# Three-part chains, 512-column builds and an earlier place for the gate tiles in the SSM stage of a hybrid encoder step

## The chip, the cores and the metric

The kernel runs on one core of a Trainium2 chip. The metric is the device time of one execution in microseconds (us), the median of several runs. TensorE multiplies matrices, VectorE (DVE in the rows) and GpSimd (POOL) work elementwise, ScalarE (ACT) does activations and copies out of PSUM, and SyncE (SP) issues the DMAs.

## The reference, cut to what matters

One layer is applied to 1024 prompt tokens and 32 sample tokens, together 1056. After a modulated RMS norm a single wide projection gives all inputs of two branches. Branch A is a state-space model (SSM) with 32 groups of 16 channels and 64 complex states each, branch B a sparse attention whose indexer picks up to 256 keys a query. Both branches are gated and merged.

```
u, zs, q, k, v, za, qi, ki, wi, gm = jnp.split(z, offs, axis=-1)
ys, hr, hi = ssm_scan(us, h_re, h_im, disc, c_re, c_im, d_skip)   # h' = a h + b u ; y = Re(c h) + d u
ys = jax.nn.gelu(ys)
ys = ys * jax.nn.sigmoid(ys @ w_glu + b_glu)                      # GLU
ys = ys * jax.nn.silu(zs)
...                                                               # indexer, top-k selection, attention -> ya
merged = sigmoid(g_s) * (ys @ w_ps) + sigmoid(g_a) * (ya @ w_pa)  # g_s, g_a = split(gm)
out = merged @ w_o
```

## The kernel before, in words

Every large product is made in three passes over operands split in two exact parts (lines 458 to 460: high by high, low by high, high by low). `ztile` (line 464) makes 128 columns of the wide projection: it loads 512 KB of weights (line 204), splits them into a high part by a cast on ScalarE (line 46) and a low part by a subtraction on GpSimd (line 49), and runs 3 groups of 24 matmuls of 352 columns, each followed by its evacuation. The tiles of the projection differ in that evacuation alone: `uproj` (SSM input, ScalarE copies), `gate_tile` (one ScalarE tanh a group, line 490, and a store to DRAM, line 491), and `silu_tile` (a ScalarE tanh and then a VectorE product, lines 483 and 484, and a store, line 486). There are 16 gate tiles, 4 silu tiles of the SSM branch and 4 of the attention branch.

The SSM stage works in four quarters of 8 groups. `build(q)` makes the matrices of a quarter: ER and EI on VectorE (`lin`, lines 546 to 548), G2 on VectorE for quarter 0 and on GpSimd for the others (lines 558 to 560), then transposes to Bc (lines 573, 574), small products to Ksb (lines 582 to 584) and shifts to Tq (lines 589 to 593). Tokens stand in 133 chunks of 8. `chain(q)` multiplies chunk inputs Uq by Bc (line 607, "input products"), copies the result to vv (line 613), runs the rotation, the scan over chunks and the rotation back on VectorE (lines 619 to 644), which ends in the states HS, and then makes the output Yq from Uq by Tq and HS by G2 (lines 654 to 656), its gelu (lines 659 to 664) and a store to yD (line 665). vv and HS have the tag "hs" with one buffer, so they share one place in memory. Input products and output products take their PSUM tiles from one pool of two buffers (`ps_s`).

The GLU loads yD into yg (line 704), splits it (line 706) and multiplies. Behind it stand the gate tiles up to NS, the indexer, the gate tiles from NS to NI, the first `prep` of the attention, four silu tiles, the gate tiles from NI to NG, the selection of the keys on VectorE and ScalarE (lines 1001 to 1060), and the attention; gate tile 15 comes from the list `gates` inside the attention.

The instructions of an engine don't stand in the order of the text: a planner lays them out at build time by priority (the order of the text) and by its own estimate of what is ready. Each engine then runs its list strictly in order. So gate tiles 0 to 4, whose text follows the GLU, lie on TensorE ahead of it.

Of the kernel before, what the change touches and what calls it, by code (L numbers as in the profile page):

```python
# [7 lines left out]
F32 = mybir.dt.float32  # L8
# [4 lines left out]
ALU = mybir.AluOpType  # L13
PSUM = bass.MemoryType.PSUM
DRAM = bass.MemoryType.DRAM
# [7 lines left out]
NCH = 133  # L23
NST = 134
QT = [(i * 128, 128, 128 * (i + 1)) for i in range(8)]
NS, NI, NG = 5, 10, 15
# [8 lines left out]
def body(nc, tc, I, O, dbg=None):  # L35
# [3 lines left out]
    te, ve, se, ge, sp = nc.tensor, nc.vector, nc.scalar, nc.gpsimd, nc.sync  # L39
# [448 lines left out]
    def gate_tile(f):  # L488
        tg = stg.tile([128, NT], F32, tag="stg", name="tg")
        ztile(C_GM + 128 * f, 128, lambda n, ps: se.activation(tg[:, ns(n)], ps, AF.Tanh, scale=0.5))  # L490
        sp.dma_start(thD[f], tg)

# [17 lines left out]
    xq = stX.enter_context(tc.tile_pool(name="xq", bufs=1, side="right", reuse_waits="tile"))  # L510
    fl = lambda t, k: t[:, k].rearrange("p a b -> p (a b)")

    P1, P2 = (xq.tile([128, 2, 16, 8], F32, name=n) for n in ("P1", "P2"))
    C1, C2 = (xq.tile([128, 2, 16, 16], F32, name=n) for n in ("C1", "C2"))
    for e in range(2):
        r = slice(64 * e, 64 * e + 64)
        for d in range(2):
            o = slice(64 * d, 64 * d + 64)
# [9 lines left out]
    def build(q):  # L528
# [13 lines left out]
        def lin(eng, out, a, b, c, d, op):  # L542
            for k in range(4):
                e1, e2 = (xq.tile([128, 16, 8], F32, name="e" + x, tag="e" + x + ("v" if eng is ve else "g"), bufs=2)
                          for x in "12")
                eng.tensor_tensor(e1, a[:, k], b[:, k], op=ALU.mult)
                eng.tensor_tensor(e2, c[:, k], d[:, k], op=ALU.mult)
                eng.tensor_tensor(out[:, k], e1, e2, op=op)
# [4 lines left out]
        e3 = [128, 16, 8]  # L553
        for g in range(8):
            k, e = 4 * q + g // 2, g % 2
            e1, e2 = (xq.tile(e3, F32, name="e" + x, tag="e" + x + ("v" if eng is ve else "g"), bufs=2) for x in "12")
            for o, pt_, ct in ((e1, P1, C1), (e2, P2, C2)):
                eng.tensor_tensor(o, pt_[:, e, k].unsqueeze(1).to_broadcast(e3),
                                  ct[:, e, k].unsqueeze(2).to_broadcast(e3), op=ALU.mult)
            eng.tensor_tensor(G2[:, g], e1, e2, op=ALU.add)  # L560
# [35 lines left out]
    def chain(q, ops):  # L596
        Uq, G2, Bc, Tq = ops
        pr = slice(4 * q, 4 * q + 4)
# [10 lines left out]
        vv = xq.tile([128, 2, 4, NST], F32, name="vv", tag="hs")  # L609
        for c in range(2):  # L610
            for e in range(2):
                s_ = slice(64 * (c ^ e), 64 * (c ^ e) + 64)
                se.copy(vv[64 * e:64 * e + 64, c, :, 0:NCH], va[e][s_].rearrange("p (k c) -> p k c", k=4)[:, :, 0:NCH])
        vr4, vi4 = vv[:, 0, :, 0:NCH], vv[:, 1, :, 0:NCH]
# [33 lines left out]
        Yq = xq.tile([128, 8, NCH], F32, name="Yq", tag="uy", bufs=2)  # L648
# [19 lines left out]
    ops = build(0)  # L668
    for q in range(4):
        if q < 3:  # L670
            uproj(q + 1)
        nxt_ = build(q + 1) if q < 3 else None
        chain(q, ops)
        ops = nxt_
    for q in range(4):
        silu_tile(C_ZS + 128 * q, zsD[q])
# [31 lines left out]
    for q in range(4):  # L708
# [5 lines left out]
        for n in range(3):  # L714
            c = ns(n)
# [8 lines left out]
    for f in range(NS):  # L724
        gate_tile(f)
    stG.close()

# [543 lines left out]
```

## Time and profile before

| what | us |
|---|---|
| median of 3 runs (range) | 1136.44 (1135.09 to 1136.77) |
| span of the profiled execution | 1134.5 |
| TensorE matmul busy in it | 1032.5 (91%) |
| VectorE busy | 806.0 (71%) |
| SSM stage, from the first build to the last store of yD | about 106 to 282 |
| GLU | 299 to 329 |
| indexer scores, last one | to 466 |
| selection of the keys, to the first softmax | 466 to 673 |
| attention | 673 to 972 |

A row of the profile gives time in us from the start of the span and the duration of one instruction, or for a group its busy time and mean. "Idle" is what an engine waited ahead of an instruction, with what released it. PEclk is the clock granted to TensorE as a share of full speed. Matmuls are pipelined, so their durations overlap; the step from one start to the next is the time that one costs.

### The profile page before, as it was taken

What the parts mean: (1) busy time and instruction counts of PE and PEld (TensorE: products, weight loads), DVE (VectorE), ACT (ScalarE), POOL (GpSimd) and SP (SyncE); (2) the same over time, 40 slices, a digit from 0 to 9 for tenths busy, and PEclk for the clock granted to TensorE, in tenths of its full rate; (3) what the DMA queues carried; (4) which work ended last, traced back from release to release, by engine and by line L of the source; (5) the groups of instructions that cost most, each with busy time, mean ns of one, the idle gap of its engine ahead of it and who ended that gap; (6) DMA issues with size and microseconds to landing.
All of it is one profiled execution on the core that took longest, in us unless ns stands there. A gap on an engine that the chain in (4) does not pass through costs nothing.

```text
span 1134.5 us, 17585 instructions
## 1 busy us (share of the span) xinstructions
PE 1032.5 (91%) x6298; PEld 950.9 (84%) x6298; DVE 806.0 (71%) x2001; ACT 540.3 (48%) x1141; POOL 348.1 (31%) x407
## 2 busy tenths in 40 slices
PE   7788989899799999988899969999997799999996
PEld 5477888899699889978889968999896599998775
DVE  4899986633435554899999996776857976687433
ACT  2542351343434554878778125555676666334111
POOL 2456645732412010224223203321325711220000
PEclk9999999999899999989999979999999999999999
DMA  9915121332651011333222322232243342754321
GB/s 275 231 41 153 39 58 58 115 87 88 199 155 51 22 37 59 94 95 76 81 81 95 111 80 66 75 95 57 66 120 102 106 138 86 225 175 146 122 64 51
DMA packets 128074, 115.53 MB, mean 102 GB/s; under 512 B 13500, under 2 KB 109200, under 8 KB 127988
## 3 DMA queue, kind: packets, MB, share of 16 engines
q1 hardware_dynamic: 127752, 114.36, 34.7%
q8 instruction: 50, 0.82, 0.3%
q14 instruction: 36, 0.29, 0.1%
q10 hardware_dynamic: 236, 0.06, 0.0%
HBM read 79.55 MB, written 30.08 MB: 97 GB/s over the span
## 4 chain that ended last, share of the span: by engine, by line
PE 50%; DVE 33%; ACT 6%; DMA 6%; issue 4%; SPq 1%; POOL 0%; DVEq 0%; POOLq 0%; ACTq 0%
PE pz L458 8%; PE pz L459 8%; PE pz L460 8%; DVE junk L1007 5%; ACT junkb L1005 3%; PE psm L1240 3%; PE psm L1242 3%; PE psm L1241 3%; PE pss L891 3%; PE pt L947 2%; DMA xt<-in_x_prompt 1%; PE pspo L957 1%; PE pss L786 1%; PE pss L787 1%; PE pspo L956 1%
## 5 line engine op out<-in xcount | busy, mean ns | idle before, releaser
L458 PE MATMUL pz<-hH,wh 128*128 128x352 f32 (+1 forms) x1080 | 356.6, 331 | 18.6 <-DVE zt L484 11.5
L459 PE MATMUL pz<-hL,wh 128*128 128x352 f32 (+1 forms) x1080 | 355.4, 329 | 0.1
L460 PE MATMUL pz<-hH,wl 128*128 128x352 f32 (+1 forms) x1080 | 355.4, 329 | 0.0
L49 POOL TENSOR_TENSOR wl<-raw,wh 128x1024 fp32r<-128x1024 f32 (+1 forms) x69 | 153.1, 2220 | 297.1 <-ACT wh L46 256.2
L458 PEld LDWEIGHTS pz<-hH,wh 128*128 128x128 f32 (+1 forms) x1080 | 205.7, 191 | 25.5 <-DVE zt L484 13.5
L459 PEld LDWEIGHTS pz<-hL,wh 128*128 128x128 f32 (+1 forms) x1080 | 205.7, 190 | 2.8 <-issue 0.8
L460 PEld LDWEIGHTS pz<-hH,wl 128*128 128x128 f32 (+1 forms) x1080 | 205.7, 190 | 1.9 <-issue 0.8
L1007 DVE TENSOR_SCALAR_CACHE_REDUCE junk<-sco,thra 128x1024 bf16<-128x1024 f32 (+2 forms) x96 | 96.7, 1008 | 0.4
L46 ACT CAST wh<-raw 128x1024 fp32r<-128x1024 f32 (+2 forms) x53 | 46.5, 878 | 61.7 <-PE pz L459 52.0
L895 ACT ACTIVATE Sm<-Sm,mx 128x128 f32<-128x128 f32 (+8 forms) x68 | 52.9, 777 | 44.1 <-DVE mx L892 43.7
L794 DVE SCALAR_TENSOR_TENSOR sco<-rl,wi,sco 128x384 f32<-128x384 f32 (+6 forms) x49 | 47.9, 987 | 35.0 <-ACT rl L789 34.1
L1005 ACT ACTIVATE junkb<-sco,thrb 128x896 bf16<-128x896 f32 x64 | 59.8, 934 | 19.7 <-DVE keepc L1020 10.5
L789 ACT ACTIVATE rl<-pss 128x384 f32<-128x384 f32 (+6 forms) x56 | 40.6, 737 | 49.0 <-PE pss L787 44.0
L892 DVE CUSTOM_DVE_ANT_0 Sm<-pss,mb 128x512 f32<-128x512 f32 (+4 forms) x68 | 39.9, 592 | 32.5 <-PE pt L947 27.6
L949 ACT CAST PH<-pt 128x512 fp32r<-128x512 f32 (+2 forms) x96 | 44.3, 479 | 38.0 <-PE pt L947 19.0
L950 DVE TENSOR_TENSOR PL<-pt,PH 128x512 fp32r<-128x512 f32 (+2 forms) x96 | 51.6, 550 | 8.4 <-ACT PH L949 7.1
L1242 PE MATMUL psm<-o,mL 128*128 128x512 f32 (+1 forms) x144 | 56.6, 395 | 0.0
L1240 PE MATMUL psm<-o,mH 128*128 128x512 f32 (+1 forms) x144 | 56.5, 394 | 0.0
L1241 PE MATMUL psm<-o,mH 128*128 128x512 f32 (+1 forms) x144 | 56.4, 394 | 0.0
L891 PE MATMUL pss<-kH,qs 128*128 128x512 f32 (+2 forms) x96 | 36.5, 382 | 15.1 <-DVE mx L892 14.7
L947 PE MATMUL pt<-idf,Sm 128*128 128x128 f32 x288 | 45.4, 276 | 3.3 <-DVE PL L950 3.1
L1005 ACT ACTIVATE junkb<-sco,thrc 128x384 bf16<-128x384 f32 x64 | 43.6, 681 | 7.2 <-DVE thrc L1023 3.9
(444 smaller groups left out, 2246.9 us busy)
## 6 DMA issues: line engine op xcount, KB each, us to landing
raw<-in_w_in SPq DMA_DIRECT2D x44, 512.0 KB
thD<-tg SPq DMA_DIRECT2D x16, 528.0 KB
wm<-in_w_mod SPq DMA_DIRECT2D x16, 512.0 KB
tgl<-thD SPq DMA_DIRECT2D x24, 176.0 KB
tgl<-thD SPq DMA_DIRECT2D x8, 528.0 KB
kd<-zf SPq DMA_DIRECT2D x32, 128.0 KB
raw<-in_w_mod SPq DMA_DIRECT2D x8, 512.0 KB
rawo<-in_w_o SPq DMA_DIRECT2D x8, 512.0 KB
```

The costliest lines, as they stand in the source:

```text
L49: leng.tensor_sub(l, src, f32(h))
L458: te.matmul(ps, wh, xh, start=first, stop=False)
L459: te.matmul(ps, wh, xl, start=False, stop=False)
L460: te.matmul(ps, wl, xh, start=False, stop=last)
L891: te.matmul(S[:m, :w], lhsT, r[:, c], start=t == 0, stop=t == len(rhs) - 1)
L895: se.activation(Sm[:m, :nk], Sm[:m, :nk], AF.Exp, scale=-1.0, bias=mx[:m, last:last + 1], accum_out=rs[:m])
L947: te.transpose(pt[:, (k - b0) * 128:(k - b0 + 1) * 128], P[:, k * 128:(k + 1) * 128], idf)
L1005: se.activation(junkb[:m, :nk], x[:m], AF.Sign, bias=t, accum_out=self.cnt[:m, k:k + 1])
L1007: ve.tensor_scalar(junk[:m, :nk], x[:m], t, None, op0=ALU.is_ge, op1=ALU.add, accum_out=self.cnt[:m, k:k + 1])
L1240: te.matmul(ps, mh, wh, start=first, stop=False)
L1241: te.matmul(ps, mh, wl, start=False, stop=False)
L1242: te.matmul(ps, ml, wh, start=False, stop=last)
```

## The change

The builds use whole 512-column operands where four 128-column instructions stood; each sum is made in place, the first product being written into the target. `chain` is cut into `chain_in` (input products and vv), `chain_scan` (VectorE part to HS) and `chain_out` (output products, gelu, store). The loop now runs scan(q), build(q+1), chain_in(q+1), chain_out(q), where it ran build(q+1), then the whole chain(q). vv has a buffer of its own, Yq has one buffer where it had two. Gate tiles 0 to 5 stand ahead of the silu tiles; before, gate tiles 0 to 4 stood behind the GLU. Gate tiles 6 to 10 (before 5 to 9) stand behind the indexer, 11 to 14 (before 10 to 14) ahead of the selection. Nothing else changes but comments.

```diff
-NS, NI, NG = 5, 10, 15
+NS, NI, NG = 6, 11, 15
...
         def lin(eng, out, a, b, c, d, op):
-            for k in range(4):
-                e1, e2 = (xq.tile([128, 16, 8], F32, name="e" + x, tag="e" + x + ("v" if eng is ve else "g"), bufs=2)
-                          for x in "12")
-                eng.tensor_tensor(e1, a[:, k], b[:, k], op=ALU.mult)
-                eng.tensor_tensor(e2, c[:, k], d[:, k], op=ALU.mult)
-                eng.tensor_tensor(out[:, k], e1, e2, op=op)
+            e2 = xq.tile(e4, F32, name="e2", tag="e2" + ("v" if eng is ve else "g"))
+            eng.tensor_tensor(out, a, b, op=ALU.mult)
+            eng.tensor_tensor(e2, c, d, op=ALU.mult)
+            eng.tensor_tensor(out, out, e2, op=op)
...
-        e3 = [128, 16, 8]
-        for g in range(8):
-            k, e = 4 * q + g // 2, g % 2
-            e1, e2 = (xq.tile(e3, F32, name="e" + x, tag="e" + x + ("v" if eng is ve else "g"), bufs=2) for x in "12")
-            for o, pt_, ct in ((e1, P1, C1), (e2, P2, C2)):
-                eng.tensor_tensor(o, pt_[:, e, k].unsqueeze(1).to_broadcast(e3),
-                                  ct[:, e, k].unsqueeze(2).to_broadcast(e3), op=ALU.mult)
-            eng.tensor_tensor(G2[:, g], e1, e2, op=ALU.add)
+        for e in range(2):
+            e2 = xq.tile(e4, F32, name="e2", tag="e2" + ("v" if eng is ve else "g"))
+            for o, pt_, ct in ((G2[:, e::2], P1, C1), (e2, P2, C2)):
+                eng.tensor_tensor(o, pt_[:, e, pr].unsqueeze(2).to_broadcast(e4),
+                                  ct[:, e, pr].unsqueeze(3).to_broadcast(e4), op=ALU.mult)
+            eng.tensor_tensor(G2[:, e::2], G2[:, e::2], e2, op=ALU.add)
...
-    def chain(q, ops):
+    def chain_in(q, ops):
...
-        vv = xq.tile([128, 2, 4, NST], F32, name="vv", tag="hs")
+        vv = xq.tile([128, 2, 4, NST], F32, name="vv")
...
+        return vv
+
+    def chain_scan(q, vv):
+        pr = slice(4 * q, 4 * q + 4)
...
-        Yq = xq.tile([128, 8, NCH], F32, name="Yq", tag="uy", bufs=2)
+        return HS
+
+    def chain_out(q, ops, HS):
+        Uq, G2, Bc, Tq = ops
+        Yq = xq.tile([128, 8, NCH], F32, name="Yq")
...
     ops = build(0)
+    vv = chain_in(0, ops)
     for q in range(4):
         if q < 3:
             uproj(q + 1)
-        nxt_ = build(q + 1) if q < 3 else None
-        chain(q, ops)
+        HS = chain_scan(q, vv)
+        if q < 3:
+            nxt_ = build(q + 1)
+            vv = chain_in(q + 1, nxt_)
+        chain_out(q, ops, HS)
         ops = nxt_
+    for f in range(NS):
+        gate_tile(f)
     for q in range(4):
         silu_tile(C_ZS + 128 * q, zsD[q])
...
-    for f in range(NS):
-        gate_tile(f)
     stG.close()
```

## Rows read from the trace of the kernel before

**Rows 1.** The page: busy time by engine, and the span in 40 slices.
```profile
PE 1032.5 (91%) x6298; PEld 950.9 (84%) x6298; DVE 806.0 (71%) x2001; ACT 540.3 (48%) x1141; POOL 348.1 (31%) x407
PE   7788989899799999988899969999997799999996
DVE  4899986633435554899999996776857976687433
```
**Rows 2.** Busy time by stretch: length, PE, PEld, DVE, ACT, POOL, PEclk, DMA, GB/s.
```profile
104.00:130.00 26.00, 20.59 (x132) 19.39 (x131) 25.92 (x90) 8.20 (x20) 18.82 (x35) 0.87 0.13 42
130.00:165.00 35.00, 31.23 (x219) 30.43 (x218) 32.04 (x83) 13.78 (x39) 15.05 (x22) 0.95 0.12 40
282.00:308.00 26.00, 17.97 (x98) 16.32 (x97) 11.44 (x11) 11.97 (x14) 11.87 (x5) 0.80 0.71 220
466.00:640.00 174.00, 158.79 (x957) 154.51 (x956) 168.81 (x513) 129.19 (x298) 53.19 (x34) 0.97 0.29 84
```
**Rows 3.** Waits of TensorE from 104 to 330: total us, times, longest.
```profile
PE pt L573 <- DVE ER L548: 5.4, 1, 5.4
PE pz L458 <- DVE zt L484: 4.9, 2, 4.2
PE pss L458 <- ACT wh L46: 4.3, 1, 4.3
PE pss L460 <- DVE wl L49: 3.7, 1, 3.7
PE pt L589 <- DVE Ksb L584: 2.7, 1, 2.7
PE pss L655 <- DVE HS L643: 2.6, 2, 1.7
PE pt L573 <- DVE EI L548: 2.3, 4, 1.0
```
**Rows 4.** Chain that ended last, from the last SSM quarter to the GLU: start, us.
```profile
249.35 0.62 DVE w L619
...
263.90 0.72 PE pss L655 x4
...
281.64 0.36 SPq L665
282.10 7.41 DMA yg<-yD
289.58 8.36 ACT ygH L46 x7
```
**Rows 5.** Timeline between quarters 1 and 2 of the chain: start, us, engine.
```profile
200.70 0.39 PE L655 MATMUL pss<-HS,G 128*128 128x133 f32 x2
203.97 1.98 PE L607 MATMUL pss<-Uq,Bc 128*128 128x133 f32 x16
207.63 0.73 DVE L619 TENSOR_TENSOR w<-vv,TCt 128x532 f32<-128x532 f32 x1 [3.04 <-ACT vv L613]
...
225.04 0.71 DVE L644 TENSOR_TENSOR HS<-gr,gi 64x536 f32<-64x536 f32 x1
```
**Rows 6.** Timeline of TensorE in the GLU.
```profile
305.23 0.50 PE L458 MATMUL pss<-ygH,wh 128*128 128x352 f32 x1
305.52 0.50 PE L459 MATMUL pss<-ygL,wh 128*128 128x352 f32 x1
```
**Rows 7.** Timeline of TensorE around the end of the selection.
```profile
663.08 0.32 PE L459 MATMUL pz<-hL,wh 128*128 128x352 f32 x1
663.24 0.32 PE L460 MATMUL pz<-hH,wl 128*128 128x352 f32 x1
672.95 0.80 PE L891 MATMUL pss<-kH,qs 128*128 128x512 f32 x1 [9.39 <-DVE mx L892]
```
**Rows 8.** Groups from 105 to 300, shapes apart: count, busy us, mean ns.
```profile
L558 POOL TENSOR_TENSOR e<-P,C 128x128 f32<-128x128 f32 x47 | 31.0, 687 | 1.2 <-DVE C L522 1.2
L560 POOL TENSOR_TENSOR G<-e,e 128x128 f32<-128x128 f32 x24 | 15.8, 678 | 0.2
L662 POOL TENSOR_TENSOR a<-a,Yq 128x532 f32<-128x532 f32 x8 | 10.7, 1332 | 0.5
L548 DVE TENSOR_TENSOR ER<-e,e 128x128 f32<-128x128 f32 x16 | 6.0, 403 | 2.6 <-PE pt L582 2.6
L619 DVE TENSOR_TENSOR w<-vv,TCt 128x532 f32<-128x532 f32 x4 | 3.3, 824 | 3.0 <-ACT vv L613 3.0
```
**Rows 9.** Timeline of one collision of VectorE with GpSimd.
```profile
107.06 2.38 POOL L49 TENSOR_TENSOR wl<-raw,wh 128x1024 fp32r<-128x1024 f32 x1
107.17 2.42 DVE L546 TENSOR_TENSOR e<-RR,BR 128x128 f32<-128x128 f32 x1
```
**Rows 10.** Timeline of ScalarE: second groups of two gate tiles, then two groups of prep(1).
```profile
629.04 0.47 ACT L490 ACTIVATE tg<-pz 128x352 f32<-128x352 f32 x1 [3.37 <-PE pz L460]
640.56 0.46 ACT L490 ACTIVATE tg<-pz 128x352 f32<-128x352 f32 x1 [3.32 <-PE pz L460]
...
659.76 0.45 ACT L834 COPY zf<-pz 128x352 f32<-128x352 f32 x1 [2.54 <-PE pz L460]
674.42 0.42 ACT L834 COPY zf<-pz 128x352 f32<-128x352 f32 x1
```
**Rows 11.** By tile, ER and then tg: ns min/median/max, first and last start.
```profile
L548 DVE TENSOR_TENSOR ER<-e,e x16: 275/290/1343, 111.1 to 158.1; 128x128 f32<-128x128 f32 x16
L490 ACT ACTIVATE tg<-pz x48: 437/462/469, 217.0 to 656.8; 128x352 f32<-128x352 f32 x48
```

More of the change, by code (lines that the diff above doesn't have):

```diff
@@ L594, in build @@
         return Uq, G2, Bc, Tq
-    def chain(q, ops):
+    def chain_in(q, ops):
         Uq, G2, Bc, Tq = ops
-        pr = slice(4 * q, 4 * q + 4)
         va = [ps_s("va"), ps_s("vb")]
```

## The prediction

> **What bounds the kernel now.** I read the page first: TensorE is busy for 91% of the span, and only in the slices ahead of 150 us and near 290, 490, 660 and 870 us does its share drop [rows 1]. So the end of the kernel is TensorE's work plus the time in which it waits or runs slowly, and a change in the SSM stage is worth what it removes of that lost time, not what it removes from VectorE's busy time. The busy time by stretch says which engine is late in each stage: from 104 to 130 us VectorE has no free time (25.9 of 26 us) and TensorE's clock is 0.87; from 282 to 308 us TensorE works for 18.0 of 26 us at a clock of 0.80 while no other engine reaches half; from 466 to 640 us, in the selection, VectorE has 168.8 of 174 us [rows 2]. The waits of TensorE from 104 to 330 us name what was late: two waits at the start of the GLU (4.3 and 3.7 us, together 8.0), one for a silu tile's VectorE product (4.9 us in two, the longest 4.2), one for ER (5.4), then Ksb (2.7), HS (2.6) and EI (2.3) [rows 3].
>
> The chain of waits shows why the GLU is late. The last output products of the chain begin at 263.9, the store of yD is issued at 281.6, its way through DRAM takes 7.4 us and the splits on ScalarE 8.4 us [rows 4]. So from HS to the GLU's first matmul some 34 us pass (264 to 298), and the last scan decides when. The period of the quarters comes from the timeline: output products of quarter 1 end at 200.7, input products of quarter 2 follow at 204.0, and its scan begins at 207.6 after VectorE has stood for 3.0 us [rows 5]. vv waits for HS's place and the input products for the PSUM tiles that the output products hold.
>
> **The change, part by part.** The sum is made against the profiled span, 1134.5 us; the median of the runs is 1.9 us above it, and I add that at the end.
>
> *Chains in three parts, vv apart from HS.* This takes the output products, the gap and the input products out of the ring that connects one scan to the next. The scan of quarter 2 begins at 207.6 and ends with HS at 225.8 [rows 5], that of quarter 3 begins at 249.4 [rows 4]: a period of 42 us, of which the scan is 18. What stays in the ring is the scan, the next build's VectorE part (six instructions of 0.82 us, 5 us, [rows 8]) and, where it isn't done by then, part of the copy to vv. I estimate a period of 24 to 28 us, so that the last scan ends 42 to 54 us earlier (three periods, each 14 to 18 us shorter) and yD is split well before 270. What is late next is TensorE itself: it has ten projection tiles to run there. So the two GLU waits go, 8.0 us [rows 3]; between 0, if the period does not shrink, and 8.0 I take 8.0, since even a period shorter by only 5 us (three periods, 15 us) brings the splits 15 us forward and the extra tile below lasts 11.5. The slow matmuls behind these waits go with them: starts are 0.29 us apart there [rows 6], about double the 0.16 us apart at 663 [rows 7], and over some 15 matmuls that is 2.0 us. What the split adds: Yq has one buffer, so the copies of the next quarter wait for the store of this one, 7.4 us by the yD transfer [rows 4] against a period of over 20; nothing.
>
> *Builds in 512 columns.* VectorE runs 96 instructions of 128 columns for ER and EI, at 403 ns in the row shown, and 24 such for G2 of quarter 0; 24 and 6 of 512 columns replace them. The nearest row is the 532-column product at 824 ns [rows 8]: 96 times 0.40 is 38, 24 times 0.82 is 20, so 18 us of VectorE time leave the stretch 104 to 165. GpSimd has 71 instructions for G2 in the trace, 31.0 and 15.8 us together; 18 of the 532-column kind at 1.33 us [rows 8] are 24 us instead of 47. Both are off TensorE's path except where TensorE waits for ER, EI, Ksb: 10.4 us [rows 3]. Of the 5.4 us for ER I take nothing, since the first transposes now wait for three whole 512-column instructions (3 times 0.82, 2.5 us, and one collision of 2.4 us [rows 9], about the 5 us of today). Of Ksb and EI together, 5.0 us, between 0 and 5.0, I take half, 2.5, because they stand in VectorE's list behind scans and shorter builds halve the queue but don't empty it. The clock dips in the two stretches to 165 us, 0.87 and 0.95 [rows 2], lose 26 times 0.13 plus 35 times 0.05, 5.1 us; they follow the waits, so I take 1.5 of it.
>
> *Gate tiles ahead of silu tiles.* A gate tile leaves PSUM through ScalarE alone, a silu tile needs VectorE, whose list runs in order and holds scans. With gates as the filler of the scans the longest wait of this kind goes, 4.2 us [rows 3], and I keep 0.7 for silu tiles that run beside the last scan; bounds 0 and 4.9. The silu tiles now end just ahead of the GLU, so the stores of zsD and the loads of z2 on SP's queue lie closer; the GLU needs z2 one quarter at a time and the first quarter's store is three tiles old by then, so nothing.
>
> *One gate tile moves from the selection to the SSM stage.* It brings one 512 KB load, one cast, one GpSimd split of 2.4 us (a collision with VectorE that the period's slack covers), 72 matmuls, three tanhs and a store. On TensorE a tile takes 11.5 us (640.56 less 629.04) [rows 10]. In the SSM stage this is work, not loss. In the selection it leaves 11.5 us of TensorE time free, and TensorE already stands for 9.4 us there until the first softmax [rows 7], because VectorE sets the end of that stage. The first group of the next prep's K tile runs ahead of that stand and the second at 674 [rows 10], so 48 matmuls of that tile (7.6 us) and the next tile can fill the hole, if the planner puts them there. Bounds: 0 if all is filled, 11.5 if nothing is. It was already placing such work there, so I take 3.0.
>
> Sum: 8.0 + 2.0 + 2.5 + 1.5 + 4.2 = 18.2 us less lost time, 3.0 given back: 15.2. The span becomes 1119.3, and with 1.9 the time **1121 us**.
>
> **The rivals.** *Longer GpSimd instructions hold up VectorE.* A VectorE product that starts 0.1 us behind a GpSimd split of 2.38 us takes 2.42 us and ends with it [rows 9], where such products have a mean of 0.4 [rows 8]. If every one of the 18 GpSimd products of 1.33 us does this to an instruction that TensorE waits for, the four kinds of waits on ER, EI, Ksb and HS, eight in number [rows 3], grow by up to 0.9 us each (1.33 less the 0.4 of a 128-column one), 7.5 us, and the 4.0 us taken for Ksb, EI and clock are gone too: 1121 + 11.5, about **1133**. Against it: the total that GpSimd holds falls from 47 to 24 us. The Trainium skill, "SBUF — State Buffer", section "SBUF: two separate sides", says that the port pair shared by the two engines is an exclusive lock held for a whole instruction; by that rule fewer and longer holds mean rarer but worse waits, and the trace agrees with the lock (2.42 against 2.38 us).
>
> *The hole in the selection stays open* (the slower side). The planner may leave TensorE without the K tile there. Then the full 11.5 us are lost against whatever the SSM stage gives back; it decides from the point where the SSM stage gives less than 11.5. If only the GLU waits of 8.0 go, the time is 1136.4 - 8.0 + 11.5, **about 1140**. For it speak the present stand of 9.4 us, which the planner did not foresee, and VectorE's full stretch there [rows 2], which fixes the length of the selection whatever TensorE does.
>
> *The planner makes nearly the same plan.* Gate tiles whose text stood behind the GLU already ran ahead of it, from 217 us, and the last of the four builds has its ER by 158 us, 90 us ahead of its scan [rows 11]. If the order of text decides little, the tile and the waits change places and the time stays at **1135 to 1138**.
>
> *More goes.* If VectorE's 18 us in 104 to 165 also shorten the ER wait and all dips, another 5.4 + 3.6 + 2.5, and the hole is filled: **1107**.
>
> **How the numbers follow.** Forecast 0.52 (1113 to 1128), port 0.16, hole 0.17, same plan 0.09, more 0.06. The range 1109 to 1141 takes in the forecast's bounds, the port and the hole and leaves out the far ends of the last two. A difference under about 0.2% (2.3 us) can't be told from none, so faster means below 1134.2 and slower above 1138.7. Faster: 0.52 + 0.16 + 0.06 = 0.74; same 0.09; slower 0.17.
>
> **What would show it.** In the profile of the changed kernel: vv of quarter q+1 copied before the scan of quarter q ends; scans 22 to 30 us apart; the last yD store before 250; no TensorE wait for the GLU's operands; gate tanhs between about 120 and 210, and no TensorE wait on a silu product over 1 us; the first softmax 10 to 18 us earlier than 673, and more than one group of prep(1)'s K tile ahead of it. I am wrong if the first softmax isn't earlier, or if it is and TensorE's stand ahead of it has grown to 15 us or more; or if scans stay 35 us apart, which would mean that memory or PSUM, not the order, sets the period.

## The result, and the profile after

The changed kernel takes 1145.51 us (median of 4 runs, 1144.66 to 1146.52) where the kernel before takes 1136.33 us in the runs beside it: a ratio of 1.0075, with a 95% interval from 1.0054 to 1.0095. The forecast was 1121 us with a range of 1109 to 1141, so the sign is wrong and the time lies above the range. The profiled execution has a span of 1142.8 us, 8.3 us more than the 1134.5 us of before.

The page of the changed kernel, the busy time by engine and the slices of TensorE and VectorE, hardly differs from [rows 1]:

```profile
PE 1039.4 (91%) x6298; PEld 954.5 (84%) x6298; DVE 815.6 (71%) x1911; ACT 541.9 (47%) x1142; POOL 335.4 (29%) x352
...
PE   7878888988999999988989969899997899999997
...
DVE  4899898814334564799999996776858976587433
```

The same 6298 matmuls run, so the question is where they wait or run slowly. Busy time by stretch of the kernel after (columns as in [rows 2]), with the selection shifted by the 10 us that it now comes later:

```profile
104.00:130.00 26.00, 16.12 (x102) 15.77 (x102) 23.14 (x37) 4.99 (x10) 14.15 (x14) 0.80 0.13 42
130.00:165.00 35.00, 31.79 (x233) 31.10 (x232) 34.50 (x56) 16.98 (x44) 17.48 (x18) 0.98 0.21 65
...
285.00:330.00 45.00, 44.97 (x281) 43.79 (x280) 17.53 (x23) 10.64 (x20) 6.24 (x3) 1.00 0.37 121
476.00:650.00 174.00, 158.78 (x958) 154.46 (x957) 169.14 (x516) 130.33 (x299) 51.85 (x33) 0.97 0.29 85
```

VectorE executes 37 instructions from 104 to 130 us instead of the 90 of [rows 2] and is still busy for 23.1 us of the 26. From 104 to 165 us VectorE is busy for 57.6 us where it was for 58.0. TensorE has lost in the first of these stretches: it is busy for 16.1 us instead of 20.6, at a granted clock of 0.80 instead of 0.87. The GLU, in the stretch from 285 us, now runs without a gap at full clock (44.97 of 45 us), where [rows 2] had a clock of 0.80. The selection is as full of VectorE as before (169.1 against 168.8 us). So the forecast gain at the GLU came, and something as large went elsewhere. The waits of TensorE from 104 to 330 us (total, times, longest), to be read beside [rows 3]:

```profile
PE pt L569 <- DVE rh L630: 9.9, 1, 9.9
PE pss L657 <- ACT Yq L659: 6.1, 3, 3.0
PE pt L585 <- DVE Ksb L580: 3.2, 1, 3.2
PE pz L458 <- DVE zt L484: 3.1, 1, 3.1
PE pt L569 <- ACT vv L608: 1.4, 1, 1.4
PE pss L658 <- DVE HS L642: 0.4, 1, 0.4
```

Both waits of 4.3 and 3.7 us at the GLU are gone and those on HS nearly so. In their place stand one wait of 9.9 us ahead of the first transposes of ER (5.4 before) and three on the copies to Yq, 6.1 us, which did not exist. Together the waits listed make 24.1 us; those of [rows 3] made 25.9.

The three-part chain itself did what it should. The last HS comes at 228.1 us (264.6 before), the last store of yD is issued at 251.5 (281.6, [rows 4]), and the scans end at 147.5, 178.0, 201.8 and 228.1. But nothing behind it is earlier, as the marks of the two executions show (us; "tile matmuls left" are those 352-column matmuls of the projection tiles, of 3240 in all, that have not started by the first softmax):

| mark | before | after | difference |
|---|---|---|---|
| last matmul of the GLU | 328.0 | 336.6 | +8.6 |
| last indexer score | 465.9 | 476.1 | +10.2 |
| first softmax | 672.6 | 680.5 | +7.9 |
| first product of the attention branch of the merge | 975.9 | 981.9 | +6.0 |
| end of the span | 1134.5 | 1142.8 | +8.3 |
| tile matmuls left at the first softmax | 600 | 551 | -49 |
| from the first softmax to the end | 461.9 | 462.3 | +0.4 |

The GLU ends 8.6 us later because exactly 72 more tile matmuls, one gate tile of 11.5 us, have run ahead of its end (1056 against 984) and only 2.9 us were gained against that. And the last two lines are the other half: by the first softmax 49 more matmuls are done, at 0.16 us each [rows 7] 7.8 us of TensorE time, and the rest of the kernel takes as long as before.

### The profile page after: what moved, and what is told of

It is laid out like the page before. It is cut to its first block, busy times and chain, and to the rows that moved or that the text cites. A ratio compares the mean times of both kernels' runs of the same rounds, so it can differ in the third digit from the quotient of the medians.

```text
span 1142.8 us, 17424 instructions
## 1 busy us (share of the span) xinstructions
PE 1039.4 (91%) x6298; PEld 954.5 (84%) x6298; DVE 815.6 (71%) x1911; ACT 541.9 (47%) x1142; POOL 335.4 (29%) x352
## 4 chain that ended last, share of the span: by engine, by line
PE 54%; DVE 30%; DMA 6%; ACT 5%; issue 4%; POOL 1%; SPq 0%; DVEq 0%; POOLq 0%; ACTq 0%
PE pz L458 9%; PE pz L459 9%; PE pz L460 9%; DVE junk L1014 4%; PE pss L898 3%; PE psm L1247 3%; PE psm L1249 3%; PE psm L1248 3%; ACT junkb L1012 2%; DMA xt<-in_x_prompt 2%; PE pt L954 2%; PE pspo L964 1%; PE pss L793 1%; PE pss L794 1%; PE pspo L963 1%
## 5 line engine op out<-in xcount | busy, mean ns | idle before, releaser
L49 POOL TENSOR_TENSOR wl<-raw,wh 128x1024 fp32r<-128x1024 f32 (+2 forms) x69 | 153.6, 2227 | 285.0 <-ACT wh L46 268.8
L898 PE MATMUL pss<-kH,qs 128*128 128x512 f32 (+2 forms) x96 | 37.9, 396 | 18.4 <-DVE mx L899 14.7
L1230 ACT ACTIVATE tt<-xo 128x512 f32<-128x512 f32 (+1 forms) x18 | 11.4, 632 | 75.5 <-DVE xo L1228 46.4
```

The source lines that it names most:

```text
L49: leng.tensor_sub(l, src, f32(h))
L898: te.matmul(S[:m, :w], lhsT, r[:, c], start=t == 0, stop=t == len(rhs) - 1)
```

## Experiments

Two theories were put against each other. **Tile theory:** the gate tile moved ahead of the GLU costs its 11.5 us there and is not paid back where it was taken away. **Chain theory:** the new order or the longer instructions of the SSM stage cost the time. In the expectations below, "theory A" is the tile theory and "theory B" or "waits theory" the chain theory; "plan theory" says that a wait taken away is replaced by others, so that their sum stays. Ratios are to the kernel before on the same chip, with 95% intervals. Marks and waits are read from one profiled execution of each kernel. Most of these lie within 2.6 us of the median of their kernel; that of the wide builds for quarters 1 to 3 is 5.2 us above it and that of the kernel without tile 0 is 3.9 us below.

**The gate tile back in its place.** The changed kernel with the numbers of tiles of before:

```diff
-NS, NI, NG = 6, 11, 15
+NS, NI, NG = 5, 10, 15
```

> The changed kernel with gate tile counts as before (5 ahead of the silu tiles, 5 behind the indexer, tile 10 again in the selection). Theory A, the moved tile: in the changed kernel the GLU ends 8.6 us later, which is 11.5 us of one more gate tile less about 3 us of saved waits, and later stages give back only about 2 of the 11.5; so this kernel ends its indexer 10 to 12 us earlier than the changed one and measures 1135 to 1139. Theory B, the waits: the tile is work moved and is repaid by work pulled ahead of the first softmax (48 matmuls, 7.6 us); the loss comes from new TensorE waits in the SSM stage (ER 9.9, Yq 6.1, a silu product 3.1 us); so this kernel measures 1142 to 1146.

Measured: 1136.49 us, ratio 0.9984 [0.9964, 1.0003]. The whole loss is gone with this one line: from 1.0075 to 0.9984 is 0.91%, 10.3 us. The GLU ends at 323.5 us, 13.1 earlier than in the changed kernel and 4.5 earlier than before. So the rest of the change is worth 4.5 us there, where the forecast had 18.2, and at the end of the kernel not even that can be told from nothing. The first softmax comes 7.7 us earlier than before (664.9 against 672.6), with 631 tile matmuls left instead of 600, and the rest takes 7.2 us longer. Its two largest waits of TensorE in the same stretch are those of the changed kernel; of the two waits at the GLU, one is still there (3.5 us):

```profile
PE pt L569 <- DVE rh L630: 8.7, 1, 8.7
PE pss L657 <- ACT Yq L659: 5.3, 2, 2.8
PE pss L460 <- DVE wl L49: 3.5, 1, 3.5
PE pt L585 <- DVE Ksb L580: 3.2, 1, 3.2
...
PE pt L569 <- DVE EI L546: 1.2, 1, 1.2
PE pz L458 <- DVE zt L484: 0.7, 1, 0.7
PE pss L658 <- DVE HS L642: 0.4, 1, 0.4
```

**The gate tile alone moved**, in the kernel before:

```diff
-NS, NI, NG = 5, 10, 15
+NS, NI, NG = 6, 11, 15
```

> The kernel before with the gate tile counts of the change alone (6 behind the GLU in the text, 5 behind the indexer, 4 ahead of the selection). Theory A: the tile costs 11.5 us ahead of the indexer, of which the stand of 8.0 us at the GLU takes some, and little comes back: 1138 to 1146. Theory B: it is repaid: 1133 to 1138.

Measured: 1147.38 us, 1.0076 [1.0053, 1.0099]. The one line, without anything else of the change, costs 0.76%, 8.6 us. With the run before, this shows from both sides that the loss belongs to the moved tile. Its trace has the marks of the changed kernel: the GLU ends 7.1 us later than before, 551 tile matmuls are left at the first softmax, and the rest takes 465.3 us, no less than before.

**The changed kernel with the builds of before** (128-column instructions):

```diff
-            eng.tensor_tensor(out, a, b, op=ALU.mult)
-            eng.tensor_tensor(e2, c, d, op=ALU.mult)
-            eng.tensor_tensor(out, out, e2, op=op)
+            for k in range(4):
...
+                eng.tensor_tensor(e1, a[:, k], b[:, k], op=ALU.mult)
+                eng.tensor_tensor(e2, c[:, k], d[:, k], op=ALU.mult)
+                eng.tensor_tensor(out[:, k], e1, e2, op=op)
```

> The changed kernel with the builds of before in 128-column instructions. Theory B, the waits: the wait of TensorE for ER falls from 9.9 to about 5.4 us, input products of quarter 0 come some 5 us earlier, and the time falls by 4 to 7 us to 1139 to 1142. Theory A gives the builds no part in the end: 1144 to 1147.

Measured: 1144.37 us, 1.006 [1.0036, 1.0085]. The interval covers the 1.0075 of the changed kernel: inside it the width of the builds decides nothing that can be told. The wait on ER falls back from 9.9 to 5.5 us, and those on EI come to 7.7 us instead.

**The 512-column builds alone**, in the kernel before (the same edit the other way round, in `lin` and for G2):

> The kernel before with the 512-column builds alone. Theory B: the ER wait grows to about 10 us and nothing else changes, 1139 to 1142. Theory A: the builds lie beside other work, 1135 to 1138.

Measured: 1130.6 us, 0.9933 [0.9911, 0.9955], the lowest ratio of the study (the interval overlaps that of the half tiles below) and a miss for both theories, whose ranges began at 1135 and 1139. The last HS comes at 258.0 us instead of 264.6, and the GLU ends 6.0 us earlier. VectorE is busy for 50.7 us from 104 to 165 us, 7.3 less than before. This happens although TensorE's largest waits ahead of the GLU's end are

```profile
PE pt L569 <- DVE rh L627: 9.9, 1, 9.9
PE pss L458 <- ACT wh L46: 7.1, 1, 7.1
```

so the 9.9 us wait for ER belongs to the 512-column builds, not to the new chain, and the builds win in spite of it.

**The chain in three parts alone**: `chain_in`, `chain_scan` and `chain_out` with vv in its own buffer and one Yq buffer, 128-column builds, five gate tiles behind the GLU as before.

```diff
-        vv = xq.tile([128, 2, 4, NST], F32, name="vv", tag="hs")
+        vv = xq.tile([128, 2, 4, NST], F32, name="vv")
...
-        Yq = xq.tile([128, 8, NCH], F32, name="Yq", tag="uy", bufs=2)
+        Yq = xq.tile([128, 8, NCH], F32, name="Yq")
...
-        nxt_ = build(q + 1) if q < 3 else None
-        chain(q, ops)
+        HS = chain_scan(q, vv)
+        if q < 3:
+            nxt_ = build(q + 1)
+            vv = chain_in(q + 1, nxt_)
+        chain_out(q, ops, HS)
```

> The kernel before with the three-part chains, vv apart and one Yq buffer alone (builds of 128 columns, five gate tiles behind the GLU as before). Waits theory: the store of the last yD comes 25 to 35 us earlier and the GLU waits of 8.0 us go, nothing else grows: 1127 to 1132 beside a kernel before at 1136. Plan theory (each order of TensorE's list has about the same sum of waits, 22 to 26 us from 104 us to the end of the GLU, because a wait taken away lets another operand come late): GLU waits go, waits on Yq copies and builds come, 1134 to 1139.

Measured: 1141.1 us, 1.003 [1.0012, 1.0049], above both ranges. The largest term of the forecast, alone, is a loss of 0.3%, 3.4 us. The last HS is at 234.9 us, 30 us earlier than before, and the long GLU wait is gone, but the waits of TensorE are now

```profile
PE pt L573 <- DVE EI L548: 6.0, 4, 4.7
PE pt L573 <- DVE ER L548: 5.8, 2, 4.2
PE pt L589 <- DVE Ksb L584: 3.6, 2, 3.1
```

EI has grown from the 2.3 us of [rows 3] to 6.0: the builds are now late, not the scans. The GLU itself ends at 313.8 us, 14.2 earlier than before, but only because TensorE has run 98 tile matmuls fewer by then (886 against 984), which is 15.7 us of work; the first softmax comes at 672.1, as before. So an earlier GLU is no gain by itself: the work has only changed places.

**The five gate tiles ahead of the silu tiles alone:**

```diff
+    for f in range(NS):
+        gate_tile(f)
     for q in range(4):
         silu_tile(C_ZS + 128 * q, zsD[q])
...
-    for f in range(NS):
-        gate_tile(f)
```

> The kernel before with its five gate tiles ahead of the silu tiles, nothing else. Waits theory: the 4.9 us on silu products go, 1130 to 1133. Plan theory: the silu products stand closer to the GLU, whose operands are late anyway at 298 us, so TensorE has no filler left there and waits longer: 1136 to 1141.

Measured: 1137.79 us, 0.9995 [0.9982, 1.0009]: no change. The wait of 4.9 us on the silu product is gone, as forecast, and the GLU ends at 325.6 instead of 328.0. But HS has 5.4 us (2.6 in [rows 3]), and from the first softmax to the end takes 467.2 us instead of 461.9.

**The changed kernel with four gate tiles ahead of the GLU:**

```diff
-NS, NI, NG = 6, 11, 15
+NS, NI, NG = 4, 9, 15
```

> The changed kernel with four gate tiles ahead of the silu tiles and tile 9 in the selection (one tile fewer in the SSM stage than before, two fewer than the change). Tile theory: a tile ahead of the indexer costs its 11.5 us less waits, and a tile in the selection costs little as long as TensorE stands there; the GLU ends 9 to 12 us earlier than with five tiles, the selection's stand of 6 us and one group of the K tile (3.8 us) give way, so 1126 to 1132. Rival: the tile only moves and comes back whole behind the first softmax: 1135 to 1138.

Measured: 1135.19 us, 0.9969 [0.9957, 0.9982], in the range of the rival. Between four and five tiles lies 0.15% (1.7 us, and the two intervals overlap), where the sixth cost 0.91%. The first softmax comes at 656.0 us, 8.9 earlier than with five tiles; yet 683 tile matmuls are left, and the rest takes 477.4 us, 8.3 more. Here the later stage pays for each matmul that it gets.

**Five gate tiles, and Yq in two half tiles**, each stored by itself, in the changed kernel:

```diff
-        Yq = xq.tile([128, 8, NCH], F32, name="Yq")
         for g in range(8):
+            if g % 4 == 0:
+                yh = xq.tile([128, 4, NCH], F32, name="Yq", bufs=2)
...
-        sp.dma_start(yD[q].rearrange("(g m) s c -> (m s) g c", m=16), Yq)
+                sp.dma_start(yD[q].rearrange("(g m) s c -> (m s) g c", m=16)[:, g - 3:g + 1], yh)
```

> The changed kernel with five gate tiles, and Yq in two half tiles that are each stored when ready, so that a copy no longer waits for the store of the whole last quarter. If the single Yq buffer costs what TensorE waits for it (5.3 us with five gate tiles), the wait falls under 2 us and the time by 3 to 5 us: 1131 to 1134. Plan theory: the wait goes and another takes its place, 1135 to 1138.

Measured: 1132.67 us, 0.9952 [0.9936, 0.9967]. The wait on Yq is gone and the GLU starts at 263.9 us (271.7 with whole tiles). Its end moves by 0.8 us only, 322.7 against 323.5, since other waits take the place, so the 0.3% between the two kernels (their intervals touch) is not shown as a gain of the SSM stage:

```profile
PE pt L569 <- DVE rh L630: 8.7, 1, 8.7
PE pt L585 <- DVE Ksb L580: 5.5, 2, 3.2
PE pz L458 <- DVE zt L484: 4.5, 2, 2.7
```

**The 512-column builds for quarters 1 to 3 only**, in the kernel before, to take the 9.9 us wait away:

```diff
+            if q == 0:
+                for k in range(4):
+                    e1, e2 = (xq.tile([128, 16, 8], F32, name="e" + x, tag="s" + x) for x in "12")
...
+                return
```

> The kernel before with 512-column builds for quarters 1 to 3 and the 128-column build for quarter 0, whose operands TensorE waits for. If the long wait for ER (9.9 us with 512 columns throughout, 5.4 before) is a plain addition, this kernel is 3 to 5 us faster than the one with 512 columns throughout: ratio 0.988 to 0.991 to the kernel before. Plan theory: the first wait shortens and others come, ratio 0.992 to 0.997.

Measured: 1141.66 us, 1.004 [1.0021, 1.0059], a miss: 1% slower than with the wide builds everywhere. The edit is not quite the 128-column build of before: its two temporaries have one buffer each where that build had two. The wait on ER is still 8.4 us, since the first product of ER starts at 110.1 us (106.4 before), behind three copies that take 1.1, 2.5 and 1.2 us instead of 0.3 to 0.4. In the timeline of VectorE the scan of quarter 0 begins at 134.0 us (129.4 with wide builds everywhere), behind 128-column pieces of G2, and two of its instructions take 2.8 us instead of 0.7:

```profile
133.78 0.29 DVE L565 TENSOR_TENSOR G<-e,e 128x128 f32<-128x128 f32 x1
133.99 0.70 DVE L630 TENSOR_TENSOR w<-vv,TCt 128x532 f32<-128x532 f32 x1
...
135.35 2.80 DVE L632 TENSOR_TENSOR gr<-w,w 128x532 f32<-128x532 f32 x1
...
151.49 2.77 DVE L654 TENSOR_TENSOR HS<-gr,gi 64x536 f32<-64x536 f32 x1
```

Beside each of these two stands a GpSimd split, in the timeline of GpSimd:

```profile
135.07 2.50 POOL L49 TENSOR_TENSOR wl<-raw,wh 128x1024 fp32r<-128x1024 f32 x1 [4.42 <-ACT wh L46]
...
151.30 2.38 POOL L49 TENSOR_TENSOR wl<-raw,wh 128x1024 fp32r<-128x1024 f32 x1 [7.78 <-ACT wh L46]
```

That scan ends at 155.0 us instead of 147.1, the later ones follow 36 to 38 us apart (35 to 38 with the wide builds everywhere), and the last HS is 9.2 us later. That the 8 us at the first scan are the cause of the 1% was read from the traces and not tried by itself.

**The parts that had helped together**: five gate tiles, Yq in halves, 128-column build for quarter 0.

```diff
...
+            if q == 0:
+                for k in range(4):
...
+                return
```

> The changed kernel with five gate tiles, half stores of Yq, and the 128-column build for quarter 0. By plain addition the ER wait falls from 8.7 to about 5 us: ratio to the kernel before 0.990 to 0.993 (it was 0.995 with the 512-column build throughout). Plan theory: 0.994 to 0.998.

Measured: 1131.25 us, 0.9959 [0.9942, 0.9976]. It can't be told from the half tiles alone (0.9952), nor is it better than the wide builds alone.

**A gate tile left out**, once the first, which runs ahead of the GLU, and once number 14, whose text stands ahead of the selection. The kernel before computes nothing for that tile and stores zeros in its place:

```diff
-        ztile(C_GM + 128 * f, 128, lambda n, ps: se.activation(tg[:, ns(n)], ps, AF.Tanh, scale=0.5))
+        if f == 0:
+            ge.memset(tg, 0.0)
+        else:
+            ztile(C_GM + 128 * f, 128, lambda n, ps: se.activation(tg[:, ns(n)], ps, AF.Tanh, scale=0.5))
```

> The kernel before with gate tile 0 left out (its 72 matmuls, load and splits; zeros are stored in its place), a measurement of what a tile costs ahead of the indexer. Tile theory: 11.5 us of TensorE time there moves the indexer and with it the selection; the kernel is 7 to 11 us faster. Rival, that TensorE has time for one tile beside the waits of the SSM stage: 0 to 4 us faster.

Measured without tile 0: 1134.76 us, 0.9978 [0.9962, 0.9994], a gain of 2.5 us, below the 7 to 11 of the tile theory and within the 0 to 4 of the rival: what a tile costs ahead of the GLU depends on how many there are. A sixth cost 8.6 us on balance, and leaving out one of the five gives back 2.5. The wait at the head of the GLU grows,

```profile
PE pss L458 <- ACT wh L46: 14.6, 1, 14.6
```

where the two waits there made 8.0 us in [rows 3] and now make 18.3 with the 3.7 us behind it. Its first matmul is bound to the operands, which come 7.6 us earlier (the last split ends at 290.5 instead of 298.1), not 11.5. The GLU ends 7.8 us earlier and the first softmax comes 12.7 us earlier; then 4.9 us are lost again up to the attention branch of the merge, with 631 matmuls left.

> The kernel before with gate tile 14 left out, the last ones of the selection, and zeros stored in its place: what a tile costs there. Tile theory: VectorE sets the length of the selection, the K tile of the next prep is pulled ahead, and the attention has a floor at about 600 tile matmuls behind the first softmax, so nothing comes of it: the kernel is 0 to 3 us faster. Rival, TensorE bounds both stages: 8 to 11.5 us faster.

Measured without tile 14: 1135.7 us, 0.9984 [0.9969, 0.9999], a gain of 1.8 us. This is the price of a gate tile in the group from which the change takes one: 11.5 us of TensorE work less, and hardly a sixth of it is seen at the end. The first 77 us of the attention of this kernel show what TensorE does with the time: 443 matmuls, clock 0.94.

```profile
670.90:748.00 77.10, 70.95 (x443) 65.35 (x443) 55.86 (x154) 42.49 (x98) 20.63 (x30) 0.94 0.23 60
```

## Why the prediction was wrong, and where it was right

**Two steps failed.** The forecast was a gain of 15.2 us, the result is a loss of 9.2 us: 24.4 us between them. The gate tile, taken at 3.0 us, accounts for 5.6 to 7.3 of it. The sum of the SSM stage, taken at 18.2 us, accounts for about 16: with the tile back in its old place the changed kernel is 0.16% faster than before, 1.8 us, and its interval includes no difference at all. The second error is the larger one; the first is why the result is a loss and not a tie.

**The gate tile: "In the SSM stage this is work, not loss", with 3.0 us given back.** It measured 8.6 us (moved alone) to 10.3 us (moved back). The step took a value near its lower bound because the next prep's K tile could fill the hole in the selection. The K tile did fill it. In the kernel after all three groups of that tile run ahead of the first softmax (ScalarE's timeline; in [rows 10] there was one at 660 and one at 674, and the third came at 682):

```profile
658.33 0.45 ACT L841 COPY zf<-pz 128x352 f32<-128x352 f32 x1 [2.54 <-PE pz L460]
662.17 0.45 ACT L841 COPY zf<-pz 128x352 f32<-128x352 f32 x1 [3.39 <-PE pz L460]
666.85 0.45 ACT L841 COPY zf<-pz 128x352 f32<-128x352 f32 x1
```

and TensorE's stand ahead of the softmax products even shrank, from 9.4 us [rows 7] to 7.4:

```profile
680.88 0.79 PE L898 MATMUL pss<-kH,qs 128*128 128x512 f32 x1 [7.44 <-DVE mx L899]
```

So the step asked the right question one stage too early. It took "the hole is filled" for "the time is paid back". The work that filled the hole was missing behind it, and that is why the time did not come back; leaving tile 14 out of the kernel before gave only 1.8 us for the same reason. The busy time of the first 77 us of the attention, in the kernel before and then in the kernel after:

```profile
672.60:750.00 77.40, 76.38 (x491) 71.55 (x491) 55.41 (x144) 42.31 (x97) 20.99 (x29) 0.96 0.26 70
```

```profile
680.50:758.00 77.50, 71.39 (x445) 65.66 (x446) 56.47 (x156) 43.08 (x99) 20.32 (x30) 0.94 0.22 59
```

Before, TensorE fills this stretch (76.4 of 77.4 us). After, it runs 46 matmuls fewer in a stretch of the same length, 7.4 us at 0.16: it stands for 6.1 us where it stood for 1.0, at a lower clock. The same view over the first 220 us, and from the first softmax to the end, before and after:

```profile
672.60:892.60 220.00, 203.07 (x1304) 186.57 (x1304) 159.21 (x396) 129.34 (x279) 77.25 (x90) 0.96 0.32 90
672.60:1134.50 461.90, 433.64 (x2576) 388.14 (x2576) 308.03 (x705) 218.96 (x469) 115.40 (x136) 0.98 0.36 106
```

```profile
680.50:900.50 220.00, 201.96 (x1255) 182.24 (x1255) 160.77 (x397) 129.17 (x276) 73.70 (x89) 0.94 0.29 81
680.50:1142.80 462.30, 431.25 (x2514) 382.09 (x2514) 310.92 (x704) 216.19 (x462) 114.20 (x135) 0.97 0.34 103
```

To the end TensorE stands for 28.26 us before and 31.05 after. So only 2.8 us of the missing work went into longer standing. The larger part went into a lower clock, 0.94 instead of 0.96 over the first 220 us (4.4 us, an estimate from these two rows).

The tile matmuls left at the first softmax are what fills the waits of the attention, and the kernels together give their price from the first softmax to the end:

| tile matmuls left | us from the first softmax to the end, by kernel |
|---|---|
| 551 | 462.3 (after), 465.3 (tile alone moved), 461.7 (after with 128-column builds), 465.2 (tile 14 left out) |
| 600 | 461.9 (before), 464.9 (chain alone), 467.2 (gates first) |
| 611 | 466.8 (wide builds but for quarter 0) |
| 631 | 469.1, 469.8, 468.3, 467.5, 468.7 (one tile back, half tiles, wide builds, best parts, tile 0 left out) |
| 683 | 477.4 (four gate tiles) |

From 551 to 600 left, 7.8 us of work, the means are 463.6 and 464.7: 1.1 us. From 600 to 631, 5.0 us of work, it is 4.0 us more, and from 631 to 683, 8.3 us of work, 8.7 us, all of it. Each value is one execution, kernels with the same number left differ by up to 5.3 us, and 683 is one kernel alone, so the place of the bend, near 600, is rough. By these traces a tile that is pulled ahead of the GLU is paid back as long as the attention keeps some 600 matmuls or more. In the changed kernel the fifth tile brought the first softmax 8.9 us later and shortened the rest by 8.3 us; the sixth brought it 15.6 us later (664.9 to 680.5, from 631 left to 551) and shortened the rest by 6.8 us only. The forecast's rows could not show this floor, but [rows 1] has the slices near 870 us, inside the attention, in which TensorE falls to 0.7; the prediction read them and didn't use them.

**The sum of the SSM stage, 18.2 us.** The GLU's end came 4.5 us earlier with the tile in its old place. There the waits show, term by term, against [rows 3], what became of the 14.7 us of waits in the sum (8.0 at the GLU, 2.5 for Ksb and EI, 4.2 for the silu tile): 4.5, 0.6 and 4.2 us went, together 9.3, and HS gave 2.2 more. ER took 3.3 us of it back and Yq 5.3, two waits that the prediction had costed at nothing:

- *Chains, 8.0 and 2.0 us at the GLU.* Right in mechanism: scans 23.8 to 30.5 us apart (forecast 22 to 30), in the changed kernel no wait for the GLU's operands and full clock there (with five tiles ahead of the GLU one of 3.5 us is left). What failed is "Yq has one buffer ... nothing". It was priced by comparing the store, 7.4 us, with the period of over 20. But the copies of the next quarter are ready right after the store is issued, since the three parts put `chain_out` of one quarter close behind that of the last. The groups of ScalarE in the kernel after show the copies idle for 16.8 us behind the store:

```profile
L659 ACT COPY Yq<-pss 128x133 f32<-128x133 f32 x32 | 8.3, 275 | 30.9 <-DMA yD<-Yq 16.8 <-PE pss L658 13.9
```

  The chain of waits gives one case: issued at 179.05, landed 4.52 us later, and the first copy of the next quarter starts at 183.7.

```profile
179.05 4.52 DMA yD<-Yq
```

  TensorE's output products wait for these copies, whose PSUM tiles they need: the 6.1 us in three of the list above. Half tiles took this wait away.
- *Builds.* "Of the 5.4 us for ER I take nothing" was off by 4.5 us, for two reasons that VectorE's timeline of the kernel after shows. First the order: the sum that completes ER (line 546) stands behind the first products of EI, two of G2, `dm` and a copy that serves the scan. Then the length: 512-column products take 1.46, 1.75 and 1.55 us while GpSimd works, and 0.68 us when it doesn't, at 118.26. The prediction's 0.82 us was a mean over the whole stretch from 105 to 300 [rows 8], not the price where the two engines work side by side.

```profile
107.78 1.46 DVE L544 TENSOR_TENSOR ER<-RR,BR 128x512 f32<-128x512 f32 x1
109.16 1.75 DVE L545 TENSOR_TENSOR e<-RI,BI 128x512 f32<-128x512 f32 x1
110.83 1.55 DVE L544 TENSOR_TENSOR EI<-RR,BI 128x512 f32<-128x512 f32 x1
112.30 2.82 DVE L554 TENSOR_TENSOR G<-P,C 128x512 f32<-128x512 f32 x1
115.05 1.44 DVE L573 TENSOR_TENSOR dm<-dsk,idf 128x128 f32<-128x128 f32 x1
116.41 1.31 DVE L625 COPY rh<-rho 128x536 f32<-128x536 f32 x1
117.66 0.68 DVE L554 TENSOR_TENSOR G<-P,C 128x512 f32<-128x512 f32 x1
...
118.26 0.68 DVE L546 TENSOR_TENSOR ER<-ER,e 128x512 f32<-128x512 f32 x1
```

  In GpSimd's timeline a product of 1.71 us starts 0.5 us ahead of the second of these, and a split of 2.78 us 0.5 us ahead of the fourth:

```profile
108.64 1.71 POOL L556 TENSOR_TENSOR G<-G,e 128x512 f32<-128x512 f32 x1
110.43 1.40 POOL L554 TENSOR_TENSOR e<-P,C 128x512 f32<-128x512 f32 x1
111.79 2.78 POOL L49 TENSOR_TENSOR wl<-raw,wh 128x1024 fp32r<-128x1024 f32 x1
```

  The transposes wait until 119.0. With 128 columns the first quarter of ER was being written from 111.1 [rows 11], and TensorE began its transposes at 111.6. The 18 us of VectorE time that were to leave 104 to 165 us did not: its busy time there fell by 0.3 us (57.96 to 57.64), because the second scan now begins at 149 us, inside this stretch; in the kernel with the wide builds alone it fell by 7.3. The forecast had multiplied mean durations of instructions that overlap, and took 0.82 us for each wide one. Half of Ksb and EI, 2.5 us, was taken as saved; in the kernel after the wait on EI is gone and Ksb has 3.2 us instead of 2.7.
- *Gate tiles ahead of silu tiles, 4.2 us.* Right in mechanism when tried alone (the 4.9 us wait goes), worth nothing at the end (0.9995), and in the whole change 3.1 us of it stayed.
- *Clock, 1.5 us.* From 104 to 130 us the granted clock fell from 0.87 to 0.80 with the longer ER wait and from 130 to 165 it rose from 0.95 to 0.98; the two nearly cancel (26 times 0.07 lost, 35 times 0.03 gained, 0.8 us lost).

**The rivals.** "The hole in the selection stays open", given 17%, had the right sign and the right cause, the moved tile, and its point of decision, a gain in the SSM stage of less than 11.5 us, is what happened. Its place was wrong: the hole closed and opened again behind the first softmax. Its 1140 us is 5.5 below the result, since it still granted the 8.0 us of the GLU waits in full. The port rival was right as to ER (collisions lengthen the wide products, three of them from 0.68 to between 1.46 and 1.75 us), but as a verdict on the change it fell: the wide builds alone have the lowest ratio of all. The Trainium skill, "SBUF — State Buffer", section "SBUF: two separate sides", describes that lock as held for a whole instruction; the 2.80 and 2.77 us beside splits of 2.50 and 2.38 us agree with it. "The same plan" fell (the order did change), and "more goes" fell.

**The signs named beforehand.** vv was copied ahead of the end of the scan for two quarters of three (142.8 against 147.5, 172.4 against 178.0; the last 2.8 us behind, 204.6 against 201.8). The last yD store was at 251.5 where 250 was named. Gate tanhs ran from 138.5 to 255, not to 210, and one wait on a silu product was 3.1 us where none over 1 was named. The scans, the GLU without a wait and the K tile ahead of the first softmax came nearly as named (scans up to 30.5 us apart, where 30 was named). The stated test of failure, a first softmax that isn't earlier, is met: it is 7.9 us later.

**What stays open.** The wide builds alone gain 0.67% and the rest of the change, with five tiles, adds nothing on top of them but loses some: 0.9984 with it. The chain alone loses 0.30%, and the waits that it brings are named above. Why the wide builds and the split chain together don't reach the wide builds alone is only partly shown: the half tiles of Yq give 0.9952, but that interval touches the one without them, and the rest was not separated. Why the 4.5 us that the GLU gains with the tile in its old place are not seen at the end was read from the traces only (31 more tile matmuls left at the first softmax, 7.2 us more behind it). Whether another order of the same tiles would move the bend near 600 was not tried. Nor was it tried to give TensorE other work during the 9.9 us wait for ER.

## What to carry to other kernels

Work moved ahead as filler is free only if the engine has free time where it goes to, or if the stage that it comes from is bound by that engine and ends earlier without it. This must be followed to the end of the program: a hole that is filled with later work is only moved, until a stage is reached where that engine has no free time. When one wait is removed from an engine that runs its list in order, sum all its waits over the stage and not the one: here the list changed in every line and the total only went from 25.9 to 24.1 us. A buffer taken away is to be priced by when its next writer is ready under the new order, not by the mean period.

## What the hardware showed that was not expected

A 512-column VectorE product takes 0.68 us undisturbed and 1.46 to 1.75 us beside GpSimd products of the same width, and one of 512 to 536 columns that started within about 0.5 us of the start of a GpSimd split took 2.8 to 2.9 us, in all six cases from 104 to 300 us in the traces of before and after. So a list of a few long instructions can be as late as one of many short ones: from 104 to 130 us VectorE is busy for 23.1 us with 37 instructions and was for 25.9 us with 90.
